# Mixture of softmaxes: unit 0 in one load, the first exponentials of units 0 and 1 in the output tile, and unit 1 waiting head by head

## Chip, cores, metric

One core of one Trainium2 chip. The metric is the device time of one execution in microseconds (us); the median of a kernel's runs is quoted, with the lowest and highest.

## The reference

```python
batch, seq, vocab, num_heads = 32, 128, 4096, 4      # logits: (32, 128, 4, 4096) float32
prior_probs = softmax(prior, axis=-1)                # (32, 128, 4), cut: written out with exp, max, sum
softmax_    = softmax(logits, axis=-1)
mixture     = np.sum(prior_probs[..., None] * softmax_, axis=2)      # (32, 128, 4096)
```

So 268.4 MB are read, 67.1 MB written.

## The kernel before

The 4096 rows are 32 units of 128 rows. A unit is one load of 8 MiB into half of `ltile`, four exponentials on ScalarE with their row sums, one coefficient per row and head, one multiply and three multiply-adds on VectorE into half of `obuf`, and one store of 2 MiB. Loads go out from ScalarE's queue, stores from SyncE's (the last five from ScalarE's). The waits are written by hand (`only(ins, *what it waits for)`).

```python
def load(u):
    if u == 0 or u >= U - 3:
        cuts = (0, 2, 3, 4) if u == U - 1 else (0, 2, 4)    # unit 0: two halves
    else:
        cuts = (0, H)
    ...
        if u >= 2:   # half of ltile is free after the multiply of two units ago
            only(ld, adds[u - 2, 0] if h == 0 else exps[u - 2, to - 1])
# in the loop over units (cut)
es = (lt[:, 0], ebuf1, ebuf2, ebuf3)       # where the four exponentials go
...
if bufd and u and h in (1, 2):             # exponential 2 waits for add 1 of the unit before,
    keep += (adds[u - 1, 1 if h == 1 else H - 1],)          # exponential 3 for its last add
...
exp(h, *(free if sets[0][1] == H and h == H - 1 else ()))   # exponential 4 waits for store u-2
```

"Exponential 1 to 4" are the heads 0 to 3; `adds[u, 0]` is the multiply, `adds[u, 1..3]` are adds 1 to 3. The next load is issued on ScalarE just ahead of the next unit's first exponential.

The softmax here doesn't subtract the row's maximum and nothing guards it: scores larger than these inputs give would overflow.

## Time and profile before

| | before |
|---|---|
| time | 780.76 us (780.73 to 780.80, 3 runs) |
| VectorE, ScalarE busy | 66%, 61% of the span |
| transfers | 335.64 MB, 431 GB/s over the span, 433 in the middle |
| first exponential, load 4 issued, unit 31's first exponential | 12.25, 82.51, 749.04 us |

A row of such a table is read as a place on one time axis: the transfer engines are full from about 1 us to 777, so every instant in the middle is also a count of bytes moved. The lines themselves stand in the prediction.

### The profile page before, as it was taken

The numbers are of one execution on the slowest core, as the hardware profiler recorded it, in microseconds if no ns is written. First come the engines' busy times: TensorE is split into PE (matmuls) and PEld (weight loads), VectorE is DVE, ScalarE is ACT, GpSimd is POOL, SyncE is SP. The second block draws the span as 40 slices with busy tenths as digits, with TensorE's granted clock in tenths as the row PEclk, the third lists the DMA queues.
The fourth block names the chain that finished last, engine by engine and source line by source line (L and its number), as shares of the span: only waits on it lengthen the run. The fifth ranks groups of instructions, "written<-read, shape, count | busy, mean of one in ns | idle before, by whom it ended". The sixth has DMA issues, their size and how long they took to land.

```text
span 779.1 us, 620 instructions
## 1 busy us (share of the span) xinstructions
DVE 517.7 (66%) x175; ACT 472.2 (61%) x258; POOL 7.6 (1%) x41
## 2 busy tenths in 40 slices
DVE  2447865568655686556875558755577555788986
ACT  4376555765557755577555675556755567557782
POOL 0000000000000000000000000000000000000000
DMA  9999999999999999999999999999999999999998
GB/s 407 458 417 400 475 404 431 431 465 424 404 468 401 463 417 423 452 448 414 417 468 407 458 404 468 421 413 448 416 459 417 457 405 464 410 429 431 432 428 379
DMA packets 10131, 335.64 MB, mean 431 GB/s; under 512 B 1136, under 2 KB 1136, under 8 KB 1168
## 3 DMA queue, kind: packets, MB, share of 16 engines
q10 hardware_dynamic: 6048, 276.83, 82.2%
q1 hardware_dynamic: 4080, 58.79, 17.6%
q14 instruction: 3, 0.02, 0.0%
HBM read 268.50 MB, written 67.11 MB: 431 GB/s over the span
## 4 chain that ended last, share of the span: by engine, by line
DMA 60%; DVE 28%; ACT 9%; issue 2%; POOL 0%; DVEq 0%; ACTq 0%; POOLq 0%
DMA out_dram<-obuf 47%; DVE obuf L200 23%; DMA ltile<-in_logits_dram 13%; ACT ebuf L176 8%; DVE obuf L194 4%; DVE ltile L200 1%; ACT ltile L176 1%; POOL coeff L187 0%; DVE rden L185 0%; DVEq L271 0%; ACTq L111 0%; POOLq L271 0%; ACTq L176 0%
## 5 line engine op out<-in xcount | busy, mean ns | idle before, releaser
L200 DVE SCALAR_TENSOR_TENSOR obuf<-ebuf,coeff,obuf 128x4096 f32<-128x4096 f32 x90 | 403.6, 4484 | 3.8 <-POOL coeff L187 0.6
L176 ACT ACTIVATE ebuf<-ltile 128x4096 f32<-128x4096 f32 x90 | 324.1, 3601 | 33.3 <-DVE obuf L200 19.4
L176 ACT ACTIVATE ltile<-ltile 128x4096 f32<-128x4096 f32 x38 | 137.4, 3615 | 255.4 <-DMA ltile<-in_logits_dram 255.0
L185 DVE RECIPROCAL rden<-dsum 128x4 f32<-128x4 f32 (+2 forms) x37 | 6.4, 174 | 235.9 <-ACT ebuf L176 233.2
L194 DVE TENSOR_SCALAR obuf<-ltile,coeff 128x4096 f32<-128x4096 f32 x30 | 70.6, 2353 | 10.9 <-POOL coeff L187 10.9
L200 DVE SCALAR_TENSOR_TENSOR ltile<-ltile,coeff 128x4096 f32<-128x4096 f32 (+1 forms) x7 | 27.0, 3874 | 1.0 <-POOL coeff L187 0.9
L176 ACT ACTIVATION_READ_ACCUMULATOR ebuf<-ltile 128x1 f32 x90 | 16.8, 187 | 0.0
L187 POOL TENSOR_TENSOR coeff<-rden,pp 128x4 f32<-128x4 f32 (+2 forms) x37 | 7.4, 201 | 756.2 <-DVE rden L185 745.6
L176 ACT ACTIVATION_READ_ACCUMULATOR ltile<-ltile 128x1 f32 x38 | 7.1, 186 | 0.0
L194 DVE TENSOR_SCALAR ltile<-ltile,coeff 128x4096 f32<-128x4096 f32 x2 | 4.7, 2353 | 0.6 <-POOL coeff L187 0.6
L153 ACT ACT_TABLE_LOAD x1 | 1.3, 1283 | 2.2 <-issue 2.2
L151 DVE TENSOR_REDUCE pmax<-pr 32x128 f32<-32x512 f32 x1 | 0.7, 674 | 2.5 <-DMA pr<-in_prior_dram 2.5
L162 DVE STREAM_TRANSPOSE pp<-pn 32x256 f32<-32x256 f32 x4 | 1.7, 435 | 0.1
L154 DVE TENSOR_REDUCE pmax<-pr 32x128 f32<-32x512 f32 x1 | 0.7, 674 | 0.7 <-ACT pr L153 0.7
L156 DVE TENSOR_TENSOR pn<-pr,pmax 32x512 f32<-32x512 f32 x1 | 1.0, 1019 | 0.0
L155 DVE RECIPROCAL pmax<-pmax 32x128 f32<-32x128 f32 x1 | 0.9, 941 | 0.0
L153 ACT ACTIVATE pr<-pr 32x512 f32<-32x512 f32 x1 | 0.6, 628 | 0.5 <-DVE pr L152 0.5
L152 DVE TENSOR_TENSOR pr<-pr,pmax 32x512 f32<-32x512 f32 x1 | 0.7, 679 | 0.0
L260 POOL MEMSET const-bfloat16-1.0<- 128x1 bf16 x1 | 0.1, 102 | 0.0
L260 POOL MEMSET const-uint8-127<- 128x1 uint8 x1 | 0.1, 102 | 0.0
L260 POOL MEMSET const-float32-0.0<- 128x1 f32 x1 | 0.1, 99 | 0.2 <-issue 0.2
L260 POOL MEMSET const-float32-1.0<- 128x1 f32 x1 | 0.1, 99 | 0.0
## 6 DMA issues: line engine op xcount, KB each, us to landing
out_dram<-obuf SPq DMA_DIRECT2D x28, 2048.0 KB, 28.1
ltile<-in_logits_dram ACTq DMA_DIRECT2D x7, 4096.0 KB, 25.5
ltile<-in_logits_dram ACTq DMA_DIRECT2D x2, 2048.0 KB, 30.9
out_dram<-obuf ACTq DMA_DIRECT2D x2, 2048.0 KB, 26.6
out_dram<-ltile ACTq DMA_DIRECT2D x1, 2048.0 KB, 19.3
out_dram<-ltile ACTq DMA_DIRECT2D x2, 1024.0 KB, 4.8
ltile<-in_logits_dram ACTq DMA_DIRECT2D x28, 29.6
pr<-in_prior_dram SPq DMA_DIRECT2D x1, 64.0 KB, 2.5
```

The lines of the kernel that those rows point to most:

```text
L151: nc.vector.reduce_max(pmax, pr, axis=AX.X)
L152: nc.vector.tensor_sub(pr, pr, pmax.unsqueeze(2).to_broadcast([2 * G, P, H]))
L153: nc.scalar.activation(pr, pr, AF.Exp)
L154: nc.vector.reduce_sum(pmax, pr, axis=AX.X)
L155: nc.vector.reciprocal(pmax, pmax)
L156: nc.vector.tensor_mul(pn.rearrange("k h r -> k r h"), pr, pmax.unsqueeze(2).to_broadcast([2 * G, P, H]))
L162: nc.vector.transpose(pp[32 * t : 32 * (t + 1), :, :, c : c + 2 * G], pq[:, :, :, 32 * (t % 2) : 32 * (t % 2 + 1)],)
L176: ex = nc.scalar.activation(es[h], lt[:, h], AF.Exp, accum_out=dsum[:, u, h : h + 1])
L185: rc = nc.vector.reciprocal(rden[:, u, h : h + n], dsum[:, u, h : h + n])
L187: mul = nc.gpsimd.tensor_mul(coeff[:, u, h : h + n], rden[:, u, h : h + n], ppu[:, h : h + n])
L194: st = nc.vector.tensor_scalar(out=acc[:, lo:hi], in0=es[h][:, lo:hi], scalar1=coeff[:, u, h : h + 1], scalar2=None, op0=ALU.mult,)
L200: st = nc.vector.scalar_tensor_tensor(out=acc[:, lo:hi], in0=es[h][:, lo:hi], scalar=coeff[:, u, h : h + 1], in1=acc[:, lo:hi], op0=ALU.mu ...
```

## The change

Its intent: loads 2 and 3 no longer wait for VectorE's multiply, because the first exponential no longer sits in the load's own buffer; unit 0 needs one transfer fewer; and unit 1, which would meet busy buffers, waits for each buffer by itself.

```diff
-        if u == 0 or u >= U - 3:
+        if u >= U - 3:
...
-            if u >= 2:
+            if u in (2, 3):
+                only(ld, exps[u - 2, H - 1])
+            elif u > 3:
                 only(ld, adds[u - 2, 0] if h == 0 else exps[u - 2, to - 1])
...
-            es = (lt[:, 0], ebuf1, ebuf2, ebuf3) if bufd else [lt[:, h] for h in range(H)]
+            if bufd:
+                es = (lt[:, 0] if u > 1 else acc, ebuf1, ebuf2, ebuf3)
+            else:
+                es = [lt[:, h] for h in range(H)]
...
-                if bufd and u and h in (1, 2):
-                    keep += (adds[u - 1, 1 if h == 1 else H - 1],)
+                if bufd and u and 0 < h < (H if u == 1 else H - 1):
+                    keep += (adds[u - 1, h if h == 1 or u == 1 else H - 1],)
...
-            late = u + 2 < U - 3
+            late = 2 <= u and u + 2 < U - 3
```

The last line means that loads 2 and 3 are now issued at the end of units 0 and 1 themselves.

## The prediction

> **What bounds the kernel now.** I read the page first, for the transfers.
>
> ```profile
> span 779.1 us, 620 instructions
> DVE 517.7 (66%) x175; ACT 472.2 (61%) x258; POOL 7.6 (1%) x41
> DMA  9999999999999999999999999999999999999998
> DMA packets 10131, 335.64 MB, mean 431 GB/s; under 512 B 1136, under 2 KB 1136, under 8 KB 1168
> q10 hardware_dynamic: 6048, 276.83, 82.2%
> q1 hardware_dynamic: 4080, 58.79, 17.6%
> ```
>
> No compute engine passes 66%, while the transfer engines are full in all 40 slices. Is there any hole? Busy time by stretch (columns: stretch, length, then per engine, clock, share and GB/s of the transfers):
>
> ```profile
> 100.00:300.00 200.00, 129.75 (x42) 121.54 (x66) 1.82 (x9) 1.00 1.00 433
> 300.00:600.00 300.00, 201.34 (x63) 180.16 (x97) 2.43 (x12) 1.00 1.00 433
> 600.00:680.00 80.00, 52.53 (x17) 50.90 (x29) 0.61 (x3) 1.00 1.00 433
> 770.00:775.00 5.00, 3.25 (x2) 0.00 (x0) 0.00 (x0) 1.00 0.99 418
> 775.00:779.00 4.00, 0.00 (x0) 0.00 (x0) 0.00 (x0) 1.00 0.50 211
> ```
>
> Finer stretches place the first byte at about 1.05 us and the last at about 777.0. The 335.64 MB in those 775.9 us are 432.6 GB/s, the middle's own rate. So there is no hole worth a microsecond; outside the moving lie 1.05 us of start and 2.1 us of end (last receipt).
>
> Per unit, 8.39 MB come in and 2.10 MB go out: 10.49 MB / 433 = 24.2 us. The chain of waits looks different: it alternates "DMA out_dram<-obuf" of 28 us with about 20 us of exponential and adds. But those 28 us are not a latency that could be shortened alone: a store shares the engines with a load. From the packet counts: 28 whole loads x 128, 7 halves x 128, 2 quarters x 128, 5 stores on that queue x 128 and 42 transfers x 16 semaphore writes make 6048, so a packet is one partition's row: 64 KB for a whole load, 16 KB for a store. On one engine (433/16 = 27 GB/s) that is 2.42 us and 0.61 us. Eight row pairs, a wait behind one more load row for the store's semaphore write, and about 1.3 us of start and receipt give 8 x 3.03 + 2.42 + 1.3 = 27.9, as the chain shows. The timeline has the coupling:
>
> ```profile
> 32.18 0.33 ACTq L111 DMA_DIRECT2D ltile<-in_logits_dram  x1
> 41.31 3.62 ACT L176 ACTIVATE ltile<-ltile 128x4096 f32<-128x4096 f32 x1 [12.04 <-DMA ltile<-in_logits_dram]
> 64.51 3.62 ACT L176 ACTIVATE ltile<-ltile 128x4096 f32<-128x4096 f32 x1 [8.70 <-DMA ltile<-in_logits_dram]
> 75.90 3.60 ACT L176 ACTIVATE ebuf<-ltile 128x4096 f32<-128x4096 f32 x1
> 82.51 0.33 ACTq L111 DMA_DIRECT2D ltile<-in_logits_dram  x1
> 88.11 3.62 ACT L176 ACTIVATE ltile<-ltile 128x4096 f32<-128x4096 f32 x1 [8.51 <-DMA ltile<-in_logits_dram]
> 100.14 3.62 ACT L176 ACTIVATE ebuf<-ltile 128x4096 f32<-128x4096 f32 x1 [0.36 <-DMA out_dram<-obuf]
> ```
>
> The load of unit 2 is issued at 32.18, 9.1 us before unit 1's has landed (41.31). From unit 3 on a unit's fourth exponential waits 0.3 to 0.6 us for a store, and a load is issued 5.6 us before its predecessor lands (82.51 against 88.11). The load queue is never empty.
>
> **What the Trainium skill says.** "DMA: Bandwidth & Descriptors", section "Specifications", gives a fabric ceiling of 435 GB/s and an HBM limit of about 358 per core. The trace's 433 sides with the first. The same page, "Queues, rings and completion order", says that an engine goes round robin between its queues by packets; the 28 us above agree. "SBUF — State Buffer", "Who interferes with whom", says that DMA never contends with compute engines; this trace, at 433 GB/s beside busy VectorE and ScalarE, shows nothing against it.
>
> **The change part by part.** Unit 0's two half loads become one. No byte is saved: one transfer's 16 semaphore writes go. The tile's first exponential can't start at 12.25 any more, only when the whole unit has landed, which is where the second half lands now: 21.96. Its four exponentials take 3.61 + 3.61 + 3.61 + 3.7 = 14.5 to 14.8, so they end at 36.7 instead of 29.3: 7.4 us later. The add of unit 0 then starts at 37.3, and with 2.39 + 3 x 4.51 = 15.9 ends at 53.2 (before 45.74); store 0 goes out 7.5 us later.
>
> The first exponential goes into the output tile. Nothing is cheaper or dearer: the multiply becomes in place, and the in-place multiplies in the page take what the others do, 2353 ns. What it buys is that loads 2 and 3 need only wait for ScalarE's own last exponential, not for the multiply: the last step is 2.9 us (29.3 to 32.18 before). So load 2 goes out at 36.7 rather than 32.18, net 4.5 us later, still 4.6 before unit 1 lands at 41.3. Hidden.
>
> Unit 1 head by head: its exponentials start at 41.3 (landing unchanged), the second needs add 1 of unit 0 (44.2; free at 45.0), the third add 2 (48.7; about equal), the fourth add 3 (53.2; 0.9 us of wait). They end at 56.9 (before 55.8), and load 3 goes out then (before 58.73). Adds of unit 1 end at 73.5 (before 72.28). So the waits by head repair nearly all of unit 0's 7.4 us. With one wait for everything they would not.
>
> Unit 2 is where it bites. Load 2 lands some 2 us earlier, near 62.2, as store 0 steals fewer rows of it. But store 0, out at 53.2, lands 27.9 later, at 81.1 (before 73.6). The fourth exponential of unit 2 needs that output tile: 81.1 instead of 75.90, a new wait of some 4 us. Load 4 follows it by 6.6 to 6.9 us (100.14 to 106.77 in unit 3): issued at 87.9, 5.4 later than 82.51. Is there still something to move? Ahead of load 4 are four loads and stores 0 and 1 (store 2 is not ready before 101.5): 4 x 8.39 + 2 x 2.10 + 0.07 = 37.82 MB, at 432.6 GB/s 87.4 us, from 1.05 to 88.5. Load 4's first byte comes about 1 us after issue (as at the start), 88.9. Expected hole: 0.4 us, uncertain by 1.5 either way; before, the reserve was 88.5 - 83.5 = 5 us. The load queue itself runs dry near 85, but store 1 fills the gap.
>
> After that each unit has the loop last add, third and fourth exponential, coefficients, adds: 3.61 + 3.74 + 2.89 + 13.56 = 23.8 us from the timeline, against 24.2 of transfers. So compute regains 0.4 us of lead per unit, holes can't repeat by much, and late in the run the old picture returns, with compute waiting for transfers. A lost transfer microsecond, though, is never regained.
>
> The end, from the timeline:
>
> ```profile
> 729.61 3.62 ACT L176 ACTIVATE ltile<-ltile 128x4096 f32<-128x4096 f32 x1 [2.35 <-DMA ltile<-in_logits_dram]
> 739.33 3.62 ACT L176 ACTIVATE ltile<-ltile 128x4096 f32<-128x4096 f32 x1 [2.41 <-DMA ltile<-in_logits_dram]
> 749.04 3.62 ACT L176 ACTIVATE ltile<-ltile 128x4096 f32<-128x4096 f32 x1 [2.40 <-DMA ltile<-in_logits_dram]
> ```
>
> The last half loads land 9.7 us apart, 4.19 MB at 432 GB/s: alone and gapless, as the stores of units 28 and 29 are queued behind them. So 749.04 is only the time at which a fixed number of bytes has moved, whatever the phase between loads and stores, and the last 30 us (unit 31's exponentials, adds and stores) follow at a fixed distance. The end moves by exactly the hole. Sum: 780.76 - about 0.0 (the 16 writes) + 0.4, rounded up to 781.1 since a hole can be long but not negative.
>
> **The rivals.**
> A: no hole at all, the time is unchanged within 0.3 us (780.5 to 781.0). For it: the full rows of transfers, and an estimate of the hole smaller than its error. About as likely as mine.
> B: compute becomes the bound of the first units. With only 0.4 us of slack per unit, a loss of 5.4 us of lead could leave the queues dry two or three times, on 16 engines not at the same moment. For it: the loop of 23.8. Against it: between two load issues there is always 24.2 us of bytes. It would make 782 to 784.
> C: a gain. Load 3 goes out 1.8 us earlier and unit 0's rows are whole. Against it: neither queue was ever empty, and the only idle time is 3.1 us at the two ends, which the change doesn't touch. At most 0.5 us: 780.3. To pass 2% would need 15.6 us.
>
> **Range and chances.** Runs before spread by 0.07 us, another chip or session perhaps 0.3. From C's 0.5 below to B's lower half above: 780.0 to 782.5. 2% either way is 15.6 us, five times all idle transfer time on the one side, and three times all of load 4's delay on the other, so faster 0.01, slower 0.01.
>
> **What would show it.** In the new timeline: first exponential near 21.9; unit 1's still at 41.3; load 3's issue near 57; the fourth exponential of unit 2 near 81 with a wait for a store of about 4 us; load 4's issue near 88; transfers with a dip (or none) around 88 and otherwise 433 GB/s; unit 31's first landing at 749.0 plus the hole. I am wrong if the middle rate is no longer 433, if holes come back in unit after unit, or if 749 moves by other than the end does.

## The result

The changed kernel took 783.60 us (782.83 to 784.74, 6 runs), the kernel before 780.75 (780.60 to 780.82, 6 runs): a ratio of 1.0037, 95% interval 1.0024 to 1.0050. It is slower by 2.85 us (0.4%, but clear of the noise), outside the predicted 780.0 to 782.5, and its own runs scatter over 1.9 us where those of before scatter over 0.2. A ratio is the mean time of one kernel's fast runs over that of the other's of the same rounds, so not quite the ratio of the medians.

The page of the changed kernel:

```profile
span 781.7 us, 620 instructions
DVE 517.6 (66%) x175; ACT 472.0 (60%) x258; POOL 7.6 (1%) x41
DMA  9999999999999999999999999999999999999998
```

Nothing here tells of 2.6 us: the engines' work is the same, and the transfers are full in every slice. The timeline of its first 90 us is more use (start, duration, instruction, and what ended the idle time before it):

```profile
22.23 3.62 ACT L182 ACTIVATE obuf<-ltile 128x4096 f32<-128x4096 f32 x1 [17.87 <-DMA ltile<-in_logits_dram]
36.76 0.33 ACTq L111 DMA_DIRECT2D ltile<-in_logits_dram  x1
41.56 3.62 ACT L182 ACTIVATE obuf<-ltile 128x4096 f32<-128x4096 f32 x1 [4.82 <-DMA ltile<-in_logits_dram]
56.95 0.33 ACTq L111 DMA_DIRECT2D ltile<-in_logits_dram  x1
80.91 3.62 ACT L182 ACTIVATE ebuf<-ltile 128x4096 f32<-128x4096 f32 x1 [3.81 <-DMA out_dram<-obuf]
87.52 0.33 ACTq L111 DMA_DIRECT2D ltile<-in_logits_dram  x1
87.91 3.62 ACT L182 ACTIVATE ltile<-ltile 128x4096 f32<-128x4096 f32 x1 [3.29 <-DVE obuf L202]
113.92 3.62 ACT L182 ACTIVATE ltile<-ltile 128x4096 f32<-128x4096 f32 x1 [5.53 <-DMA ltile<-in_logits_dram]
```

Every instant is where the prediction put it within half a microsecond: first exponential 22.23, load 2 at 36.76, unit 1 at 41.56, load 3 at 56.95, the new wait for store 0 ending at 80.91, load 4 at 87.52. Unit 3 at 87.91 then waits for the multiply ahead of the load in ScalarE's own queue, not for a transfer: load 3 has already landed. Unit 4's data is there at 113.9, against 112.28 before. From there on the delay grows to its final size, and the last lap shows it:

```profile
751.56 3.62 ACT L182 ACTIVATE ltile<-ltile 128x4096 f32<-128x4096 f32 x1 [2.40 <-DMA ltile<-in_logits_dram]
```

That is 2.52 us after the 749.04 of before, and the span ended 2.6 later. Where did the transfers lose it? Transfers by stretch, before and then changed (the last two columns are the busy share of the 16 engines and GB/s):

```profile
70.00:200.00 130.00, 82.18 (x26) 81.93 (x45) 1.01 (x5) 1.00 1.01 438
200.00:680.00 480.00, 319.68 (x100) 290.83 (x159) 4.05 (x20) 1.00 1.00 433
```

```profile
70.00:200.00 130.00, 83.27 (x26) 77.12 (x44) 1.01 (x5) 1.00 1.00 427
200.00:680.00 480.00, 319.65 (x100) 291.18 (x159) 4.04 (x20) 1.00 1.00 434
```

Between 70 and 200 us the engines are as busy as before and move less. After 200 us the rate is the old one. In these tables a packet counts where it starts, so a stretch is uncertain by about one 64 KB row on 16 engines, 1.05 MB or 8 GB/s over 130 us. Spreading each packet's bytes over its own time is sharper: at 90.25 us both kernels have moved the same 37.97 MB, at 200 us 85.55 and 84.94 MB, at 740 us 319.64 and 319.04. So 0.61 MB, 1.4 us at 433 GB/s, are lost between 90 and 200 us, and nothing around the suspected hole.

For more I went to the trace's packet records, which have start, duration, size and queue of each packet, without the engine's number. A packet is one partition's row: 64 KB for a whole load, 16 KB for a store. Three quantities come out of them:

- Empty time: how far the number of packets in flight falls short of 16, between 10 and 740 us, averaged over the 16 engines.
- Long rows: packets of 64 KB that took over 2.6 us, where the rest take 2.42; counted after 70 us.
- Landing times per engine: each load ends with one 4-byte semaphore write per engine. For the first half of unit 31's load, when every engine has moved the same bytes in every kernel, I list the mean of the 16 writes and the last one. The mean says how much engine time was lost; the difference of the two says how far one engine lags.

```
                       empty us  long rows   unit 31, first half: mean  last    end of transfers
before                  0.05       0                             747.82  748.55   777.85
changed                 0.06      40                             749.20  751.15   780.38
```

There is no hole. The mean engine lost 749.20 - 747.82 = 1.38 us, in rows that took longer, up to 3.8 us, though never idle: what the rows started between 70 and 200 us took above their usual times sums to 1.4 us per engine, against 0.0 before. The rest, (751.15 - 749.20) - (748.55 - 747.82) = 1.22 us, is lag: in the kernel before the 16 writes of a whole load lie within 1.0 us of each other all along; in the changed kernel they do until load 3 (0.6 us), and from load 4 on they lie 2.5 to 3.4 us apart. Compute needs all 16, so it waits for the last. The sum is the 2.6 us.

### The profile page after: what moved, and what is told of

Same layout as the page of the kernel before. It is cut to its first block, busy times and chain, and to the rows that moved or that the text cites. A ratio compares the mean times of both kernels' runs of the same rounds, so it can differ in the third digit from the quotient of the medians.

```text
span 781.7 us, 620 instructions
## 1 busy us (share of the span) xinstructions
DVE 517.6 (66%) x175; ACT 472.0 (60%) x258; POOL 7.6 (1%) x41
## 4 chain that ended last, share of the span: by engine, by line
DMA 53%; DVE 32%; ACT 11%; issue 3%; POOL 0%; DVEq 0%; ACTq 0%; POOLq 0%
DMA out_dram<-obuf 43%; DVE obuf L208 26%; DMA ltile<-in_logits_dram 10%; ACT ebuf L182 10%; DVE obuf L202 5%; DVE ltile L208 1%; ACT obuf L182 0%; POOL coeff L195 0%; DVE rden L193 0%; DVEq L279 0%; ACT ltile L182 0%; ACTq L111 0%; POOLq L279 0%; ACTq L182 0%
## 5 line engine op out<-in xcount | busy, mean ns | idle before, releaser
L182 ACT ACTIVATE ltile<-ltile 128x4096 f32<-128x4096 f32 x36 | 130.1, 3615 | 222.6 <-DMA ltile<-in_logits_dram 218.9
L202 DVE TENSOR_SCALAR obuf<-ltile,coeff 128x4096 f32<-128x4096 f32 x28 | 65.9, 2353 | 10.4 <-POOL coeff L195 10.4
L182 ACT ACTIVATE obuf<-ltile 128x4096 f32<-128x4096 f32 x2 | 7.2, 3617 | 22.7 <-DMA ltile<-in_logits_dram 22.7
L202 DVE TENSOR_SCALAR obuf<-obuf,coeff 128x4096 f32<-128x4096 f32 x2 | 4.7, 2352 | 0.6 <-POOL coeff L195 0.6
```

The lines of the kernel that those rows point to most:

```text
L182: ex = nc.scalar.activation(es[h], lt[:, h], AF.Exp, accum_out=dsum[:, u, h : h + 1])
L202: st = nc.vector.tensor_scalar(out=acc[:, lo:hi], in0=es[h][:, lo:hi], scalar1=coeff[:, u, h : h + 1], scalar2=None, op0=ALU.mult,)
```

## The experiments

Theory L: unit 0's late start, through load 4, is the only cause. It was sharpened later to Q: a load issued about when its predecessor lands, or after, costs. All edits below are against the changed kernel unless said otherwise. "Lead" is the time from the critical load's issue to the last engine's landing of the load before it, in the profiled run.

| run | result | time, median (range) us | lead us | long rows after 70 us | unit 31: mean, last us |
|---|---|---|---|---|---|
| before | correct | 780.75 (780.60 to 780.82) | 5.2 | 0 | 747.8, 748.6 |
| changed | correct | 783.60 (782.83 to 784.74) | -0.9 | 40 | 749.2, 751.2 |
| a1_halves_back | correct | 780.83 (780.80 to 780.97) | 6.0 | 0 | 747.9, 748.6 |
| a2_one_load_alone | correct | 783.60 (783.36 to 783.90) | 1.5 (load 2) | 14 | 750.0, 751.2 |
| a3_halves_late_start | correct | 782.92 (782.04 to 785.10) | -0.9 | 26 | 748.8, 751.4 |
| a4_short_unit0 | wrong | 780.84 (780.82 to 781.52) | 5.1 | 0 | 747.8, 748.5 |
| b1_fed_early | correct | 784.28 (783.78 to 784.95) | 0.7 (load 13) | 24 | 749.8, 752.4 |
| b2_one_add_less | wrong | 780.84 (780.81 to 781.19) | 2.7 | 1 | 747.7, 748.8 |
| b3_half_add_less | wrong | 780.80 (780.75 to 783.57) | 2.1 | 0 | 747.7, 748.4 |
| b4_one_add_more | wrong | 783.81 (783.37 to 789.95) | -1.4 | 60 | 749.7, 751.3 |
| d1_wait_at_coeff | correct | 781.00 (780.92 to 781.15) | 2.9 | 0 | 747.8, 748.4 |
| d2_before_wait_at_coeff | correct | 780.93 (780.84 to 781.04) | 5.3 | 0 | 747.8, 748.5 |
| d3_late_once_midway | wrong | 785.17 (784.24 to 786.42) | -2.6 (load 17) | 62 | 751.0, 751.6 |
| c1_most_lead | correct | 782.16 (780.92 to 782.49) | 5.4 | 0 | 748.1, 749.3 |
| e1_lead_without_quarters | correct | 780.93 (780.86 to 781.03) | 5.0 | 0 | 747.8, 748.4 |
| e2_early_store0 | wrong | 780.77 (780.73 to 780.93) | 5.1 | 0 | 747.8, 748.4 |
| e3_less_late_midway | wrong | 780.94 (780.85 to 781.07) | 3.1 (load 17) | 0 | 747.9, 748.5 |

Each row has 5 timed runs or more; "wrong" results were meant to be wrong. Leads, long rows and landings are those of the one profiled run of each. The kernel before, in the same rounds, had medians of 780.80 to 780.86 (one of its runs took 782.15).

### First round: which part costs

**a1_halves_back**: only the one load is undone.

```diff
-        if u >= U - 3:
+        if u == 0 or u >= U - 3:
```

> The changed kernel with unit 0 loaded in two halves again; output-tile exponentials and head-by-head waits stay. Theory L (the loss comes only from unit 0's compute starting 9.6 us later, which makes load 4 go out about 5 us later than before and lets the 16 transfer engines fall out of step): 780.3 to 781.0 us, load 4 issued at 83 or earlier, last unit's first landing at 749.0 +-0.3. Rival W (the loss comes from the new waits and the in-place output tile): stays at 782.5 to 784.5.

Measured 780.83 us, ratio 0.9998 (0.9984 to 1.0012). The output tile and the head-by-head waits cost nothing; rival W falls. Load 4 goes out as early as in the kernel before:

```profile
82.40 0.34 ACTq L111 DMA_DIRECT2D ltile<-in_logits_dram  x1
...
88.82 3.62 ACT L182 ACTIVATE ltile<-ltile 128x4096 f32<-128x4096 f32 x1 [9.33 <-DMA ltile<-in_logits_dram]
```

**a2_one_load_alone**: the kernel before, with that one line of the change and no other.

```diff
-        if u == 0 or u >= U - 3:
+        if u >= U - 3:
```

> The kernel before with unit 0 in one load and nothing else of the change. Theory L: compute of unit 1 now also waits for the last add of unit 0 before its third exponential, so load 3 goes out near 63 us, just when load 2 lands; loss as in the changed kernel or larger, 783 to 786 us. Rival W (the waits and the output tile cost the time, not the one load): 780.5 to 781.2.

Measured 783.60 us, ratio 1.0033. One line makes the whole difference. Its timeline has the two late loads, and how close to the landing each is (a first exponential starts some 0.4 us after the last engine's landing):

```profile
39.40 0.34 ACTq L111 DMA_DIRECT2D ltile<-in_logits_dram  x1
41.31 3.62 ACT L176 ACTIVATE ltile<-ltile 128x4096 f32<-128x4096 f32 x1 [4.83 <-DMA ltile<-in_logits_dram]
...
63.18 0.34 ACTq L111 DMA_DIRECT2D ltile<-in_logits_dram  x1
...
65.73 3.62 ACT L176 ACTIVATE ltile<-ltile 128x4096 f32<-128x4096 f32 x1 [5.46 <-DMA ltile<-in_logits_dram]
```

Here load 2 is the tight one, with no store about to fill in, and load 3 follows with a lead of only 2.2 us; the empty time was 0.58 us, so part of this loss is a true hole. Load 2 has 47 long rows of its own, which the table, counting from 70 us on, leaves out. Without the output tile the lateness bites earlier, but the price is the same: the rest of the change moves the trouble from loads 2 and 3 to load 4 and saves nothing.

**a3_halves_late_start**: two halves, but compute as late as with one.

```diff
+        if u == 0 or u >= U - 3:                                      # as a1
-                keep = (loads[u, h],) + keep
+                keep = (loads[u, H - 1 if u == 0 else h],) + keep
```

> The changed kernel with unit 0 in two halves, but its first exponential made to wait for the second half, so that compute starts as late as with one load while the transfers have the old form. Theory L: like the changed kernel, 782.5 to 784.5 us, first exponential near 22, load 4 issued near 87.5. Rival R (the form of the first transfer, whole 64 KB rows which took 3.0 us instead of 2.4 at the start, is what costs): 780.4 to 781.2.

Its first exponential and load 4:

```profile
21.92 3.62 ACT L182 ACTIVATE obuf<-ltile 128x4096 f32<-128x4096 f32 x1 [17.84 <-DMA ltile<-in_logits_dram]
...
87.32 0.33 ACTq L111 DMA_DIRECT2D ltile<-in_logits_dram  x1
```

Measured 782.92 us (782.04 to 785.10), ratio 1.0030. The form of the first transfer is not it (rival R falls); the late start is. In this run the lag dominates: mean 0.97 us late, last engine 2.86 late.

**a4_short_unit0**: one load, but two adds of unit 0 left out, which pays the lateness back.

```diff
+                if u == 0 and h in (1, 2):
+                    adds[u, h] = adds[u, h - 1]
+                    return
```

> Wrong result on purpose: the changed kernel with one load, but unit 0 leaves out two of its three adds, so that store 0 goes out near 44 us instead of 53.2 and the lateness is paid back. Theory L: 780.4 to 781.2 us, load 4 issued near 82 to 83. Rival R or W (one load itself, or the output tile, costs): 782.5 to 784.5.

Measured 780.84 us. One load as such costs nothing either. Theory L stands in all four.

### Second round: how the late load costs

**b1_fed_early**: as late as the changed kernel, but the loads of units 4 to 11 go out in three parts, each once its heads are free.

```diff
+        if 4 <= u < 12:
+            return part(u, 0, 1, adds[u - 2, 0])
...
+                if 2 <= u < 10 and h >= 2:
+                    part(u + 2, 1 if h == 2 else 3, h + 1, exps[u, h])
```

> The changed kernel, equally late in its compute, but the loads of units 4 to 11 go out in three parts, each as soon as its heads are free (heads 1 and 2 after the third exponential two units before, some 10 us before the rest), so that the load queue always has rows. Theory Q (the loss comes only from the load queue running dry before a late load, which lets the 16 engines restart out of step): 780.5 to 781.3 us, and the last 16 landings of each load stay within 1 us of each other. Rival C (late compute and late stores cost the time by themselves): 782.5 to 784.5. Doubt: three parts have rows of 32 and 16 KB, which shares the engines differently with the stores.

Measured 784.28 us: missed. Through unit 11 the landings stayed within 1.5 us of each other, and there was no long row after 70 us (the rows of these loads have 32 and 16 KB). All the same, with bytes counted as above, it had moved 0.48 MB less than the kernel before by 300 us, some 1.1 us; that the small rows cost this was not tested. More is lost where whole loads return:

```profile
305.57 0.33 ACTq L121 DMA_DIRECT2D ltile<-in_logits_dram  x1
...
306.74 3.62 ACT L192 ACTIVATE ltile<-ltile 128x4096 f32<-128x4096 f32 x1 [4.08 <-DMA ltile<-in_logits_dram]
```

Load 13 goes out 0.7 us before load 12 lands (306.2 by its semaphore writes). 24 long rows follow, from 309 to 448 us, the spread of the landings goes from 1.3 us to 3.0 within two units, and by 450 us 0.85 MB are missing. The small rows also shift the shares of loads and stores, a confound that I had named. So this run decides neither for Q nor against it.

**b2_one_add_less**, **b3_half_add_less**, **b4_one_add_more**: one load, with unit 0's adds shorter by one, by a half, or longer by one.

```diff
+                if u == 0 and h == 1:                     # b2
+                    adds[u, h] = adds[u, h - 1]
+                    return
+                if u == 0 and h == 1:                     # b3
+                    hi = V // 2
+                    if u == 0 and h == 1:                 # b4: the same add again
+                        st = nc.vector.scalar_tensor_tensor(...)
+                        adds[u, h] = only(st, mul, adds[u, h])
```

> Wrong result on purpose: the changed kernel with one of unit 0's three adds left out; store 0 near 48.7 us, load 4 near 83.3, some 3.5 us before load 3 has landed. Theory Q: 780.6 to 781.3 us. Rival C (loss proportional to lateness): 782.0 to 782.5, half of the changed kernel's loss.

> Wrong result on purpose: half of one add of unit 0 left out; store 0 near 50.9 us, load 4 near 85.3, some 1.3 us before load 3 has landed, which is about the time a new load needs to its first byte. Theory Q: between the two, 780.8 to 783, and scattered from run to run. Rival C: 782.5 to 783.2.

> Wrong result on purpose: one add of unit 0 done twice; store 0 near 57.7 us, load 3 near 61.4, load 4 near 92.0, 6 us after load 3 has landed and more than store 1 can fill. Theory Q: a real hole of about 3 us besides, 785 to 788 us. Rival N (what counts is only that the engines fall out of step once, not how late load 4 is): 783 to 784.5.

Measured 780.84, 780.80 and 783.81 us. The cost is not proportional to lateness: with a lead of 2.7 us there is none, with 2.1 none in four runs of five and 2.8 us in the fifth, with -0.9 (the changed kernel) 2.85 and with -1.4 about the same, 3.0 in the median, with one run at 789.95. In b4 load 3 is late too (61.34, a lead of -0.7). b4's forecast of 785 to 788 missed, and rival N's 783 to 784.5 fits: I had load 4 at 92.0, it went out at 88.00, since store 0, with load 3 not yet issued, landed 13.8 us after its issue and not 27.7 as in the changed kernel. The tight lead of b2 in its timeline:

```profile
84.89 0.34 ACTq L111 DMA_DIRECT2D ltile<-in_logits_dram  x1
87.99 3.62 ACT L182 ACTIVATE ltile<-ltile 128x4096 f32<-128x4096 f32 x1 [6.01 <-DMA ltile<-in_logits_dram]
```

### Third round: a repair, and the same accident elsewhere

**d1_wait_at_coeff**: the wait for the store two units back moves from the fourth exponential to the coefficient multiply behind it. (**d2_before_wait_at_coeff**: the same in the kernel before.)

```diff
-                exp(h, *(free if sets[0][1] == H and h == H - 1 else ()))
+                exp(h)
-                mul = weigh(g, h + 1 - g, *(free if g == 0 and h < H - 1 else ()))
+                mul = weigh(g, h + 1 - g, *(free if g == 0 else ()))
```

> A repair of the changed kernel, correct result: the wait for the store two units back moves from the fourth exponential to the small coefficient multiply behind it, so the 3.7 us of the exponential no longer lie between the store's landing and the multiply that frees the load. Load 4 should go out near 84 us instead of 87.5, 2 to 3 us before load 3 has landed. Theory Q (a load issued after its predecessor has landed puts the 16 engines out of step for good): 780.7 to 781.3 us with at most one run in five at 783 or more, spread of the landings under 1.5 us. Rival C (late unit 0 costs by itself): 782.5 to 784.5.

> The kernel before with the same move of the wait. Theory Q: nothing left to gain since its engines are in step and its transfers full, 780.6 to 781.0 us. Rival S (the fourth exponential's wait for the store is on the path that sets the end): faster by 1 us or more, 779.8 or less.

Measured 781.00 us, ratio 1.0002 (0.9989 to 1.0016), and 780.93. This is the cleanest run: unit 0 is as late as in the changed kernel (first exponential 22.05, store 0 at 53.02), only the fourth exponential of unit 2, load 4 and what follows them are earlier.

```profile
76.82 3.60 ACT L182 ACTIVATE ebuf<-ltile 128x4096 f32<-128x4096 f32 x1
...
83.49 0.33 ACTq L111 DMA_DIRECT2D ltile<-in_logits_dram  x1
...
86.81 3.62 ACT L182 ACTIVATE ltile<-ltile 128x4096 f32<-128x4096 f32 x1 [6.30 <-DMA ltile<-in_logits_dram]
```

The fourth exponential starts at 76.82 instead of 80.91, load 4 goes out at 83.49 instead of 87.52, and the whole loss is gone. So the late compute and the late stores of units 0 and 1 by themselves cost nothing; the loss comes with the late load. In the kernel before, the moved wait gains nothing: rival S falls.

**d3_late_once_midway**, **e3_less_late_midway**: the kernel before with unit 14 alone late, by one and a half repeated adds or by a half.

```diff
+                    for end in (V, V // 2) if u == 14 and h == 1 else ():      # e3: (V // 2,)
+                        st = nc.vector.scalar_tensor_tensor(...)
+                        adds[u, h] = only(st, mul, adds[u, h])
```

> Wrong result on purpose: the kernel before, with unit 14 alone made late by 6.7 us of repeated adds, so that the load of unit 17 goes out about 1 us after the one of unit 16 has landed, as load 4 does in the changed kernel; the head is untouched. Theory Q: 782.5 to 784.5 us, spread of landings 0.8 to 1.0 us ahead of unit 17 and 2 to 4 us from there to the end. Rival H (the loss belongs to the start of the run, where queues fill): 780.7 to 781.2.

> Wrong result on purpose: the kernel before with unit 14 made late by 2.2 us instead of 6.7; the load of unit 17 goes out near 399.7 us, some 3 us before the load of unit 16 lands. Theory Q (a threshold: only a load issued at or after its predecessor's landing costs): 780.7 to 781.2 us. Rival C (cost in proportion to lateness, 4.3 us for 6.7): 782 to 782.5.

Measured 785.17 and 780.94 us. Load 17 in d3, then in e3:

```profile
403.97 0.33 ACTq L111 DMA_DIRECT2D ltile<-in_logits_dram  x1
404.35 3.62 ACT L176 ACTIVATE ltile<-ltile 128x4096 f32<-128x4096 f32 x1 [3.29 <-DVE obuf L194]
```

```profile
399.44 0.33 ACTq L111 DMA_DIRECT2D ltile<-in_logits_dram  x1
...
403.03 3.62 ACT L176 ACTIVATE ltile<-ltile 128x4096 f32<-128x4096 f32 x1 [6.50 <-DMA ltile<-in_logits_dram]
```

One late unit in the middle of the run costs no less than one at its start, and 3.1 us of lead cost nothing: rivals H and C (here: a cost in proportion to lateness) fall. d3's four loads from 17 on are all tight, with leads of -2.6, -0.1, 1.2 and 1.7 us. My forecast for d3 was 0.7 us low at the median, and its spread forecast was wrong: the landings stayed within 1.8 us of each other after unit 17. The loss there is 3.2 us of mean engine time, some 0.7 of it empty, the rest long rows. So lagging engines are a companion of a late load, not a necessary one.

**c1_most_lead**: unit 0 in four quarters, with d1's moved wait; **e1_lead_without_quarters**: halves instead of quarters; **e2_early_store0**: a1 with three quarters of one add left out, so that store 0 goes out as early as in c1.

```diff
+            cuts = (0, 1, 2, 3, 4) if u == 0 else ...      # c1;  e1: (0, 2, 4)
+                if u == 0 and h == 1:                      # e2
+                    hi = V // 4
```

> Unit 0 in four quarter loads, first exponentials of units 0 and 1 in the output tile, head-by-head waits, and the store's wait at the coefficients: the most lead of compute over transfers that these parts give. Theory Q: lead beyond what keeps the load queue fed buys nothing, 780.5 to 781.0 us. Rival S: 779.8 or less.

> The most-lead kernel with unit 0 in halves instead of quarters (output-tile exponentials, head-by-head waits and the store's wait at the coefficients stay); store 0 near 45.6 us. Theory J (the 1.3 us of the most-lead kernel came from store 0 joining the loads at 42.3 us, just after the engines had passed from load 1 to load 2, which left them one or more store rows apart): 780.7 to 781.1 us, spread of the landings under 1.1 us. Rival P (the wait at the coefficients together with the early loads does it): 782 or more.

> Wrong result on purpose: the changed kernel with unit 0 in halves and three quarters of one of its adds left out, so that store 0 goes out near 42.3 us as in the most-lead kernel, without quarter loads and with the old place of the store's wait. The load queue is never near empty. Theory J: 781.5 to 782.6 us, spread 1.5 us or more from load 2 on. Rival R (the quarters' small rows do it): 780.7 to 781.1, spread under 1.1 us.

Measured 782.16 (780.92 to 782.49), 780.93 and 780.77 us. c1 was expected to be neutral and lost 1.3 to 1.7 us in four runs of five, although its load queue is never near empty: the 16 landings of load 2 already lie 1.8 us apart, and those of later whole loads 1.3 to 2.0. Of this loss 0.8 to 1.2 us lie in the span; the rest lies outside it (time less span is 2.2 to 2.4 us in these runs, 1.8 before), and I can't say where. My theory J (the moment of store 0) fell with e2. Without the quarters the loss is gone; what about quarters puts the engines out of step stays open.

## Why the prediction was wrong

**Right: the chain of instants.** Unit 0's 7.4 us, the repair by unit 1's waits, the new wait of 3.8 us for store 0 in unit 2, load 4 at 87.5, and the dry load queue at 85 to 88 that store 1 fills. a1 confirms that the output tile and the waits are free, as stated.

**Right: the fixed tail.** In all 17 profiled kernels the last packet of loads and stores ends 29.2 to 29.3 us after the last engine's landing of unit 31's first half load, and nothing later decides.

**Wrong: "The end moves by exactly the hole."** This is the step that failed. It took the time at which fixed bytes have moved to depend only on empty time, with every 64 KB row at 2.42 us and all 16 engines abreast, as they were in the kernel before from 63 us on. In its place stand two terms that the sum did not have: long rows (1.38 us of mean engine time in the changed kernel) and a lagging engine (1.22 us).

The hole itself, 0.4 us with 1.5 either way, was in range at 0, but partly by luck, for two errors cancel. The 37.82 MB ahead of load 4 lasted until 89.9 us and not 88.5, in both kernels, since up to there the transfers move 426 GB/s and not 432.6. And load 4's first rows started from 89.66 us on, 2.1 us after its issue and not 1; until then store 1 alone kept the engines busy.

**Wrong: "holes can't repeat by much".** No hole came back, as foreseen, but the loss did: load 5 went out with a short lead too (111.31 against load 4's last landing at 113.5), and long rows appear near 92, 107, 133, 156 and 181 us, once per unit. Compute did regain its lead as foreseen (load 6 goes out 4.1 us before load 5 has landed), but the loss added up meanwhile.

**Rival B** had the size, 782 to 784, and the words "on 16 engines not at the same moment", but argued from dry queues. It was given too little weight: I let the full rows of the page stand for the full rate.

**Not settled.** Why a row takes up to 3.8 us when the load queue is about to run out. Such rows also occur where it is not: the kernel before has 32 of them, between 47 and 63 us, after its first store has joined the loads. One regularity is in the records: a load has 8 rows per engine, and by order of start 32 of the changed kernel's 40 long rows are among the last 16 of their load (all 16 of load 4, 3.10 us on average, and 10 of load 5), so the rows that lengthen are less those around load 4's late start than those at its end. Also open is why engines that have fallen out of step stay so. The records carry no engine number, and no experiment isolated either. That making a load late brings the loss about is shown (a1, a3, a4, d1 and d3 with e3); how it does so inside the transfer engines is not. Nor is lateness the only way to lose time: c1 has none.

No version beat the kernel before; the correct a1, d1, d2 and e1 equal it within 0.2 us. Its transfers leave about 3 us of empty time at the two ends and next to nothing between.

## What to carry to other kernels

In a kernel bound by transfers, what to watch is not the engines' busy share but the lead of the next load over the landing of the one before: here 2.7 us was enough, 2.1 failed in one run of five, 1.5 followed by 2.2 was not enough, and a single unit made late cost 2 to 4 us that no later slack brought back. Before dropping an early partial load, follow the delay through every buffer to the first load that it makes late. When a wait stands in front of a long instruction, see whether it can stand behind it, as the store's wait here could.

## What the Trainium skill lacked or had wrong

- "DMA: Bandwidth & Descriptors", "Specifications": the table gives the HBM limit of about 358 GB/s per core without saying when it binds (other passages of the skill do). It does not bind here: from 200 to 680 us the two kernels move 433 and 434 GB/s, near the fabric ceiling of 435 in the same table.
- The same page, "Queues, rings and completion order", has the round robin by packets, and the 28 us of a store beside a load agree. It has nothing on what it costs when one queue runs out for a while: here rows of 2.42 us became up to 3.8 us, the 16 landings of one load went from 0.6 to over 2.5 us apart and stayed so to the end, and engines that were busy throughout had moved 0.61 MB less by 200 us.
- "Perfetto Trace Analysis", "DMA Optimizations", names one case in which splitting a transfer may let the whole end sooner, "If DMA engines are generally idle". Here they never are, and splitting unit 0's load is still worth 2.8 us (780.83 against 783.60), because compute starts 10 us sooner (12.15 against 22.23). Splitting it further into quarters lost 1.2 us (782.16 against e1's 780.93).
